# Head 0's operands loaded during the scan, and fewer, alternating visits for the triangular inverses

## The chip, the cores and the metric

The kernel runs on one core of a Trainium2 chip, as one program. Its engines are TensorE (PE, with its weight loads PEld), VectorE (DVE), ScalarE (ACT), GpSimd (POOL) and SyncE (SP), which here only issues DMAs. Each runs its own instructions in order and waits at semaphores for the others; DMA engines shared by all queues move the data. The metric is the device time of one execution in microseconds. Three runs of the kernel before gave 1317.60, 1318.98 and 1319.77 us; their median is 1318.98.

## The reference

One decoder layer over 1024 tokens (16 meta tokens ahead of them), of which two parts matter here: a gated delta rule with 4 heads, computed in chunks of 64 in the reference, and an attention with 8 heads and a forget gate. Both are normalized, projected together, added to the residual, and followed by a SwiGLU block.

```python
# gated delta rule, for one sequence of chunks
a_mat = where(strict, einsum("bhncd,bhnsd->bhncs", k, k) * decay * beta[..., :, None], 0.0)
sol = triangular_solve(a_mat + eye(chunk), rhs, left_side=True, lower=True, unit_diagonal=True)
u, w = sol[..., :dv], sol[..., dv:]
# then, chunk by chunk: S_t = e^{g_t} S_{t-1} + beta_t k_t (v_t - k_t^T e^{g_t} S_{t-1})^T, o_t = S_t^T q_t

# forgetting attention: softmax with the cumulative log forget gate as a bias, in blocks of 128 queries
# out = concat(gated delta heads, attention heads) @ w_out + residual, then RMSNorm, SwiGLU, residual
```

## The kernel before

The kernel works on chunks of 128 tokens (NT = 8 of them) and keeps matrix operands as pairs of a high and a low part, so that a projection is three matmuls for each block of 128 (high x high, low x high, high x low). Intermediate results go through DRAM tensors: `rec_d` holds the delta rule's operands by chunk, `k_d` and `q_d` the attention's keys and queries by pair of heads, `c_d` its cumulative gates, `h_d` the hidden rows.

The order of PE's instructions is written by hand: a planner, `PeOrder` (`od`), keeps an estimated time and a list of chains. A chain is a generator that says when it wants to go on; whenever none is due, the planner takes the next matmul of the fill. The fill is `fox`, the projections of the attention's values, keys (`pj_fk`) and queries (`pj_fq`), later the output projection of the delta heads (`wog`, function `wout_gdn`). The planner's estimates (`od.pe`, `od.on`, the constants `LV0`, `ATT0`, `LD0`, `LEAD`) only set the order; what the chip waits for is decided by semaphores. All other engines get their instructions in the order in which the program is written out.

The stages around the change, in order of time:

- `levels(hp)`, once for each pair of heads (at 306 and at 354 us): doubles triangular inverses from blocks of 32 to 64 to 128. The products of 32x32 (`py`, `pu`, L619 and L630) use tiles of the array at rows 32b and 32b + 32, for b = 0 and b = 2. Then `up2` transposes (L644) and multiplies (L646), and `up3` multiplies again (L658), each on 64 rows, for two heads and two halves of the tokens (t0 = 0 and 4). The result goes through POOL to `rec_d`.
- `scan()` (from 375 us): `meta_state`, then `chunk(t)` for 8 chunks. Each chunk loads `ra`, `rb`, `rc`, `zt` on SP (L751 to L757, two buffers each), and runs four visits of PE: `p` (L762, needs `ra` and the state), `pvn` (L771, needs `rb`), `pd` (L781) and `po` (L789 and L790, needs `rc`). Between them DVE and ACT evict. `mkv`, the meta tokens' operand, shares the buffers of `ra`.
- `chunk_out(t)`: ACT copies `po` to `oc` and squares it, DVE, POOL and DVE make the norm's factor, DVE makes `on` (L808), PE transposes it (`ot`, L814), and ACT and DVE split it into the pair that `wout_gdn` reads.
- `attention()`: for each head, `att_head(h)` loads `kk`, `sa`, `ka`, `qa`, `avt`, `vmt` on SP (L937 to L950); `scores` multiplies into `sc` (L975, L976) with DVE's row sums (L980) and ACT's exponentials behind them; `values` transposes the probabilities (`pt`) and multiplies them with the values (`po`, L1029 to L1034). The buffers of this stage are made when the scan's have been closed.
- `wout_gdn(nb, tt)`: 12 matmuls into one PSUM bank (`wog`), an addition to a residual tile `ht` on DVE (L1128), which was loaded from the input (L1125), and a store to `h_d` on POOL (L1129). The bank is one of three in turn, until the scores of the first group are done; from there to the end of attention it is a single one, since the others are needed (`rot[0] = 0`).

Every dozen or so of projections ends with an eviction by ACT and DVE into `fhl` and a store on SP (`fox_proj`, L717).

Of the kernel before, what the change touches and what calls it, by code (L numbers as in the profile page):

```python
# [9 lines left out]
F32 = mybir.dt.float32  # L10
F32R = mybir.dt.float32r
# [20 lines left out]
GRP = 4  # L32
LV0 = (76.0, 119.0)
LAT = 0.4
ATT0 = 7.0
LEAD = 0.6
NA = 6
LD0 = (4.0, 10.0, 18.0)
CO = 3.0
RES = 6  # L40
ORDER = (0, 4, 1, 5, 2, 6, 3, 7)
# [56 lines left out]
def tile_hymba_layer(ctx, tc, x, meta, attn_norm_w, w_in, conv_w, a_log, dt_bias, gdn_norm_w,  # L98
# [22 lines left out]
    def ps_t(name):  # L121
        return bank("tp", 3, name)
# [474 lines left out]
    def levels(hp):  # L597
# [15 lines left out]
        v4 = lambda ap: ap.rearrange("p (h t c) -> p h t c", h=2, t=NT)  # L613
        yield LV0[hp]
        py = v4(ps_s(f"py_{hp}"))
        for r, q, b in rq_:
            for i in range(2):
                for t in range(NT):
                    nc.tensor.matmul(py[r, i, t], na[q, i, t, r], u[q, i, t, q], start=True, stop=True,  # L619
                                     tile_position=(32 * b + 32, 32 * b))  # L620
                    od.pe(0.07)
# [2 lines left out]
            rdy = od.on("act", 0.5)  # L624
        yield rdy
        py = v4(ps_s(f"pu_{hp}"))
        for r, q, b in rq_:
            for i in range(2):
                for t in range(NT):
# [7 lines left out]
        lo, hi = slice(0, 64), slice(64, 128)  # L637
        t2s = {}

        def up2(i, t0):  # L640
            h = 2 * hp + i
            p2 = ps_s(f"py2_{h}_{t0}").rearrange("p (a t c) -> p a t c", a=2, t=4)
            for t in range(4):
                nc.tensor.transpose(p2[lo, 0, t], u[lo, i, t0 + t, lo], ident[lo, lo])  # L644
            for t in range(4):
                nc.tensor.matmul(p2[lo, 1, t], na[hi, i, t0 + t, lo], u[hi, i, t0 + t, hi],  # L646
                                 start=True, stop=True, tile_position=(64, 0))
            od.pe(0.7)
            t2 = lp.tile([64, 2, 4, 64], F32, tag="t2", bufs=2, name=f"t2_{h}_{t0}")
            nc.scalar.copy(t2, p2[lo])  # L650
            t2s[i, t0] = t2, od.on("act", 0.5)

        def up3(i, t0):
            h, ts = 2 * hp + i, slice(t0, t0 + 4)
            t2, _ = t2s[i, t0]
            p3 = ps_t(f"py3_{h}_{t0}").rearrange("p (a t c) -> p a t c", a=2, t=4)
            for t in range(4):
                nc.tensor.matmul(p3[lo, 0, t], t2[:, 0, t], t2[:, 1, t], start=True, stop=True,  # L658
                                 tile_position=(0, 0))
            od.pe(0.45)  # L660
# [6 lines left out]
        seq = [(i, t0) for i in range(2) for t0 in range(0, NT, 4)]  # L667
        for n, it in enumerate(seq):
            up2(*it)
            if n:  # L670
                yield t2s[seq[n - 1]][1]
                up3(*seq[n - 1])
                yield od.t + 0.3
        yield t2s[seq[-1]][1]
        up3(*seq[-1])
        lv_left.discard(hp)

    scc = ExitStack()
# [16 lines left out]
    def fox_load():  # L695
        if fox_ws:
            fox_w.append(win_block(*fox_ws.pop(0)))

    def fox_proj(dst, chunks, off, scale, nm):
        for b in range(2):  # L700
            w = fox_w.pop(0)
            for i in range(2):
                m = 2 * b + i
                for ci, (c0, n) in enumerate(chunks):
                    if (i, ci) == (0, 1):
                        fox_load()
# [12 lines left out]
    def scan():
        yield from meta_state()  # L720
        for t in range(NT):
            yield from chunk(t)

    def meta_state():
        mkv = sp.tile([P, 2, GH, P], F32, tag="ra", bufs=2, name="mkv")[:NM]
        nc.sync.dma_start(mkv, mkv_d.rearrange("h s a c -> s a h c"))
        yield od.t + 5.0
        ub = ak.tile([NM, GH, NM], F32, name="ubm")
# [178 lines left out]
    uctx.close()  # L907

    alc = ExitStack()
    al_ = alc.enter_context(tc.tile_pool(name="al", bufs=1))  # L910
# [5 lines left out]
    vmts = [al_.tile([P, P], F32R, name=f"vmt{i}") for i in range(2)]  # L916
    kas = [al_.tile([NA + DH, T], F32R, name=f"ka{i}") for i in range(2)]
    qas = [al_.tile([NA + DH, S], F32R, name=f"qa{i}") for i in range(2)]
    for ka, qa in zip(kas, qas):
        nc.gpsimd.memset(ka[:NA].bitcast(F32), 1.0)  # L920
        nc.gpsimd.memset(qa[:NA].bitcast(F32), -1.0)
    masks = []
    for z in [phm] + vmts:
        nc.gpsimd.memset(z.bitcast(F32), 0.0)

    t_ld = []

    def att_head(h):
        m, hb = h // 2, h % 2
        rows = slice(DH * hb, DH * hb + DH)  # L930
        kk = al_.tile([P, T], F32R, tag="kk", bufs=2, name=f"kk_{h}")
        sa = al_.tile([P, S], F32R, tag="sa", bufs=2, name=f"sa_{h}")
        ka, qa = kas[h % 2], qas[h % 2]
        tc_ = NM + P * GRP
        parts = ((slice(0, S // 2), slice(0, tc_)), (slice(S // 2, S), slice(tc_, T))) if h == 0 else (
            (slice(0, S), slice(0, T)),)
        nc.sync.dma_start(ka[3:NA].bitcast(F32), c_d[h])  # L937
        nc.sync.dma_start(qa[0:3].bitcast(F32), c_d[h, :, NM:T])
        for qc, kc in parts:
            for i in range(2):  # L940
                half = slice(DH * i, DH * i + DH)
                nc.sync.dma_start(kk[half, kc].bitcast(F32), k_d[m, rows, 0, kc])
                nc.sync.dma_start(sa[half, qc].bitcast(F32), q_d[m, i, rows, qc])
            nc.sync.dma_start(ka[NA:, kc].bitcast(F32), k_d[m, rows, 1, kc])
            nc.sync.dma_start(qa[NA:, qc].bitcast(F32), q_d[m, 0, rows, qc])
        vt = al_.tile([P, NT, P], F32R, tag="vt", bufs=2, name=f"avt_{h}")
        nc.sync.dma_start(vt.bitcast(F32), v_d[h, NM:T].rearrange("(t p) d -> p t d", p=P))
        vmt = vmts[h % 2]
        for r in (0, 32):
            nc.sync.dma_start(vmt[r:r + NM].bitcast(F32), v_d[h, 0:NM])  # L950
        t_ld.append(od.t)
        return m, rows, kk, sa, ka, qa, vt, vmt

    def scores(h, g, hd, out):
        m, rows, kk, sa, ka, qa, vt, vmt = hd
# [91 lines left out]

    def attention():
        groups = [(h, g) for h in range(FH) for g in range(NT // GRP)]
        hds, ptl, pos = {}, {}, [0.0]  # L1050

        def score_stream():
            for i, (h, g) in enumerate(groups):
# [3 lines left out]
                ptl[i] = []  # L1057
                for n, rdy in enumerate(scores(h, g, hds[h], ptl[i])):
                    pos[0] = i + n / (5, 9)[g]
                    yield max(rdy, t_ld[0] + LD0[i]) if i < len(LD0) else rdy  # L1060
            pos[0] = 1e9

        ss = score_stream()
# [600 lines left out]
```

## Time and profile before

| | before |
|---|---|
| median of 3 runs | 1318.98 us |
| the profiled execution | 1319.71 us |
| its span in the trace | 1318.0 us |
| granted clock of PE, mean | 0.997 |
| PE instructions | 7442 |
| DVE busy | 855.3 us |
| ACT busy | 545.4 us |
| POOL busy | 390.8 us |
| bytes moved by DMA | 233.88 MB |

The span is what the trace shows between the first and the last instruction; 1.7 us of the profiled execution lie around it. Lines of the profile (L619) are those of the kernel before. A row of the timeline gives start, duration, engine, line, operation, output and inputs, and how many instructions of one kind follow one another; in brackets stands the idle time ahead of it and what ended it. One matmul in float32 leaves more than one record, so that a group of 32 products of 32x32 has 64.

### The profile page before, as it was taken

Reading aid. Unit: us, or ns where it says so; the run is one execution under the profiler, and the core shown is the slowest. Engines: PE = TensorE matmul, PEld = TensorE weight load, DVE = VectorE, ACT = ScalarE, POOL = GpSimd, SP = SyncE. Lnnn points to the kernel's source line nnn. Section 1 sums busy time; section 2 is a strip of 40 time slices with the busy share of each in tenths; the row PEclk is TensorE's granted clock in tenths of the full one; section 3 lists DMA queues with packets and bytes.
Section 4 is the critical chain, followed back from the end, with each engine's and each line's share of the span. In section 5 each row is a group of like instructions: output and inputs, shape, how many; then the busy total and the mean of one; then the engine's idle time right before and its main releaser. Section 6 shows DMA issues by size and latency. Waiting matters only on the chain.

```text
span 1318.0 us, 20035 instructions
## 1 busy us (share of the span) xinstructions
PE 1294.8 (98%) x7442; PEld 1133.6 (86%) x7442; DVE 855.3 (65%) x1526; ACT 545.4 (41%) x918; POOL 390.8 (30%) x348
## 2 busy tenths in 40 slices
PE   8999999999999999999999999999999999999998
PEld 8999999899999988887777888888888888888887
DVE  6665789676337578996897665566566565355645
ACT  5543434232223367885553232333333343343332
POOL 2211423601013311113432644554334453010301
PEclk9999999999999999999999999999999999999999
DMA  6331743774479597647534555534444557955523
GB/s 227 100 100 45 207 140 112 203 225 148 144 235 323 185 250 219 163 115 228 171 133 137 186 176 184 160 133 157 157 165 155 176 194 264 405 183 180 209 74 128
DMA packets 184776, 233.88 MB, mean 177 GB/s; under 512 B 19120, under 2 KB 136872, under 8 KB 181864
## 3 DMA queue, kind: packets, MB, share of 16 engines
q1 hardware_dynamic: 181704, 223.70, 52.8%
q0 software_dynamic: 2976, 8.92, 2.3%
q8 instruction: 58, 0.95, 0.3%
q14 instruction: 38, 0.31, 0.1%
HBM read 154.91 MB, written 77.67 MB: 176 GB/s over the span
## 4 chain that ended last, share of the span: by engine, by line
PE 74%; DVE 9%; DMA 7%; issue 3%; ACT 3%; SPq 2%; POOL 1%; POOLq 0%; DVEq 0%; ACTq 0%
PE xp L1545 9%; PE yp L1545 7%; PE gb L1379 5%; PE ud L1379 5%; PE gd L1379 5%; PE ub L1379 5%; PE ga L1379 4%; PE ua L1379 4%; PE pj_fk L207 4%; PE pj_fq L207 3%; PE ue L1379 2%; PE ge L1379 2%; PE fv L207 2%; PE pt L1012 2%; PE po L1034 1%
## 5 line engine op out<-in xcount | busy, mean ns | idle before, releaser
L164 DVE TENSOR_TENSOR al_p<-ra_p,ah_p 128x2048 fp32r<-128x2048 f32 (+1 forms) x21 | 46.7, 2222 | 93.7 <-ACT ah_p L163 93.7
L163 ACT CAST ah_p<-ra_p 128x2048 fp32r<-128x2048 f32 (+1 forms) x21 | 37.1, 1766 | 105.8 <-PE xp L1545 48.5
L1545 PE MATMUL xp<-wh_p,al_p 128*128 128x512 f32 (+1 forms) x176 | 67.3, 382 | 0.0
L1545 PE MATMUL xp<-wl_p,ah_p 128*128 128x512 f32 (+1 forms) x176 | 67.3, 382 | 0.0
L1545 PE MATMUL xp<-wh_p,ah_p 128*128 128x512 f32 (+1 forms) x176 | 67.3, 382 | 0.0
L1432 POOL TENSOR_TENSOR gzw<-gzw,uzt 128x512 f32<-128x512 f32 x11 | 18.4, 1673 | 154.9 <-DVE uzt L1423 128.9
L1432 POOL TENSOR_TENSOR gxy<-gxy,uxy 128x512 f32<-128x512 f32 x22 | 38.9, 1766 | 66.1 <-DVE uxy L1423 45.8
L985 ACT ACTIVATE pr<-pr,sm 128x144 f32<-128x144 f32 (+3 forms) x64 | 50.5, 790 | 17.7 <-DVE sm L980 17.4
L1379 PE MATMUL gb<-uh_p,w_g_p 128*128 128x512 f32 x176 | 57.8, 389 | 0.0
L1379 PE MATMUL gd<-uh_p,w_g_p 128*128 128x512 f32 x176 | 57.8, 389 | 0.0
L1379 PE MATMUL ud<-uh_p,w_u_p 128*128 128x512 f32 x176 | 57.8, 389 | 0.0
L1379 PE MATMUL ub<-uh_p,w_u_p 128*128 128x512 f32 x176 | 57.8, 389 | 0.0
L164 DVE TENSOR_TENSOR w_u_p<-raw_u,w_u_p 128x512 fp32r<-128x512 f32 x42 | 42.8, 1018 | 21.6 <-ACT w_u_p L163 21.5
L164 DVE TENSOR_TENSOR pl<-pt,ph 128x512 fp32r<-128x512 f32 (+1 forms) x96 | 51.1, 553 | 2.2 <-ACT ph L163 1.6
L1379 PE MATMUL ga<-uh_p,w_g_p 128*128 128x512 f32 x160 | 52.5, 389 | 0.0
L1379 PE MATMUL ua<-uh_p,w_u_p 128*128 128x512 f32 x160 | 52.5, 389 | 0.0
L1545 PE MATMUL yp<-wh_p,ah_p 128*128 128x512 f32 x132 | 51.3, 389 | 0.0
L1545 PE MATMUL yp<-wl_p,ah_p 128*128 128x512 f32 x132 | 51.3, 389 | 0.0
L1545 PE MATMUL yp<-wh_p,al_p 128*128 128x512 f32 x132 | 51.3, 389 | 0.0
L163 ACT CAST ph<-pt 128x512 fp32r<-128x512 f32 (+1 forms) x96 | 44.9, 471 | 13.8 <-PE pt L1012 13.3
L164 DVE TENSOR_TENSOR wl_p<-rw_p,wh_p 128x2048 fp32r<-128x2048 f32 (+1 forms) x21 | 46.9, 2236 | 3.4 <-ACT wh_p L163 3.4
L163 ACT CAST w_u_p<-raw_u 128x512 fp32r<-128x512 f32 x42 | 26.1, 620 | 52.3 <-PE gd L1379 33.6
(646 smaller groups left out, 4305.4 us busy)
## 6 DMA issues: line engine op xcount, KB each, us to landing
ra_p<-ao_p SPq DMA_DIRECT2D x14, 1024.0 KB
raw_g<-in_w_gate_dram SPq DMA_DIRECT2D x22, 512.0 KB
raw_u<-in_w_up_dram SPq DMA_DIRECT2D x22, 512.0 KB
raw_d<-in_w_down_dram SPq DMA_DIRECT2D x22, 512.0 KB
wt_p<-raw_d SPq DMA_DIRECT2D x33, 256.0 KB
rw_p<-wt_p SPq DMA_DIRECT2D x8, 1024.0 KB
rw_p<-in_w_down_dram SPq DMA_DIRECT2D x6, 1024.0 KB
ao_p<-gzw SPq DMA_DIRECT2D x22, 256.0 KB
```

The source lines that it names most:

```text
L163: cast = nc.scalar.copy(dst_hi, src)
L164: tail[0] = (cast, nc.vector.tensor_sub(dst_lo, src, dst_hi.bitcast(F32)))
L207: nc.tensor.matmul(dst, a, b, start=first, stop=last)
L985: nc.scalar.activation(pr[:, :n], pr[:, :n], AF.Exp, bias=sm[:, np_ - 1:np_], scale=-1.0, accum_out=rsum[:, h, j:j + 1])
L1012: nc.tensor.transpose(pt[:rows_k, P * j:P * j + P], pts[j][0][:, c0:c0 + rows_k], ident)
L1034: nc.tensor.matmul(po[:, q], vt[:, kt], pl[:, q], start=False, stop=(kt == nk - 1))
L1379: nc.tensor.matmul(dst, a[:, c], b[:, k], start=(first and k == 0 and i == 0), stop=(k == 3 and i == 2), skip_group_check=not first)
L1432: last_mul[0] = G.tensor_tensor(gs[d], gs[d], us[d], op=ALU.mult)
L1545: nc.tensor.matmul(dst[:, n_], a[:, f, c], b[:, f, n_], start=(first and i == 0 and n == 0), stop=(i == NF - 1 and n == 2), skip_group_che ...
```

## The change

The loops over `py` and `pu` are turned round, so that the two blocks b = 0 and b = 2 of one product follow each other. `up2` and `up3` are cut into pieces: both halves of a head go in one visit, and the third-stage products of one head take turns with the second-stage products of the next. That makes three visits where five were.

Head 0's tiles get a pool of their own (`ale`), which is made together with the scan's; heads of odd number use a second one (`alo`), made after the scan. Head 0's loads are issued inside `fox_proj`, behind the store of the second pair's second chunk of queries, and no longer in halves. `mkv` takes a buffer of `rc` and not of `ra`. The planner's constants for the start of attention are smaller. Since `t_ld` is filled early now, all loads of `ht` take POOL's queue (`nc.gpsimd if t_ld else nc.sync`), of which the first were on SP before.

```diff
-ATT0 = 7.0
+ATT0 = 1.0
-LD0 = (4.0, 10.0, 18.0)
+LD0 = (0.0, 0.0, 10.0)
...
         py = v4(ps_s(f"py_{hp}"))
-        for r, q, b in rq_:
-            for i in range(2):
-                for t in range(NT):
+        for i in range(2):
+            for t in range(NT):
+                for r, q, b in rq_:
                     nc.tensor.matmul(py[r, i, t], na[q, i, t, r], u[q, i, t, q], start=True, stop=True,
                                      tile_position=(32 * b + 32, 32 * b))
...
+        heads = [[(i, t0) for t0 in range(0, NT, 4)] for i in range(2)]
+        for n in range(3):
+            new, old = heads[n] if n < 2 else (), heads[n - 1] if n else ()
+            p2s = [up2_t(*it) for it in new]
+            p3s = [ps_t(f"py3_{2 * hp + i}_{t0}").rearrange("p (a t c) -> p a t c", a=2, t=4) for i, t0 in old]
+            for g in range(2):
+                for t in range(4):
+                    if old:
+                        up3_m(*old[g], p3s[g], t)
+                    if new:
+                        up2_m(*new[g], p2s[g], t)
+                od.pe(0.3)
+            for it, p3 in zip(old, p3s):
+                up3_e(*it, p3)
+            for it, p2 in zip(new, p2s):
+                up2_e(*it, p2)
+            if new:
+                yield t2s[new[-1]][1]
...
                     last[0] = nc.sync.dma_start(dst(m)[:, :, c0 - off:c0 - off + n], hl[:, :, :n].bitcast(F32))
+                    if off and (m, ci) == (1, 2):
+                        assert csum_done
+                        hds[0] = att_head(0)
...
-        mkv = sp.tile([P, 2, GH, P], F32, tag="ra", bufs=2, name="mkv")[:NM]
+        mkv = sp.tile([P, 2, GH, P], F32, tag="rc", bufs=2, name="mkv")[:NM]
...
+    alec = ExitStack()
+    als = [alec.enter_context(tc.tile_pool(name="ale", bufs=1))]
     sp = scc.enter_context(tc.tile_pool(name="sp", bufs=1))
     cp = scc.enter_context(tc.tile_pool(name="cp", bufs=1, side="right"))
+    att_tiles(0)
...
-                    yield max(rdy, t_ld[0] + LD0[i]) if i < len(LD0) else rdy
+                    yield max(rdy, t_ld[h] + LD0[i]) if i < len(LD0) else rdy
```

`up2_t` is the transposes of the former `up2`, `up2_m` one product of it, `up2_e` its eviction by ACT; `up3_m` and `up3_e` are one product and the eviction of the former `up3`. `att_tiles(i)` makes the tiles `ka`, `qa`, `vmt` of a pool and clears them on POOL, as was done for both at once after the scan.

The first place is PE in the second pair of heads, the mixed visit of the levels. Names are tile names with the program's numbers; `py_3_0` are bank tiles for head 3, `t_2` the transposed pairs of head 2. Before, each visit holds one half of head 3 and the third stage of a half before it, and three projections stand between two visits:

```order
L644 MATMUL py_3_0_4073<-ident,u_3832 64x64 x4
L646 MATMUL py_3_0_4073<-u_3832,na_3825 64x64 x4
L658 MATMUL py_2_4_4084<-t_2_4_4057 64x64 x4
L207 MATMUL pj_fq_358_4012<-uh,wlo_fq_0_3733 128x342
L207 MATMUL pj_fq_358_4012<-uh,whi_fq_1_3738 128x342
L207 MATMUL pj_fq_358_4012<-ul,whi_fq_1_3738 128x342
L644 MATMUL py_3_4_4096<-ident,u_3832 64x64 x4
L646 MATMUL py_3_4_4096<-u_3832,na_3825 64x64 x4
L658 MATMUL py_3_0_4107<-t_3_0_4082 64x64 x4
```

Now it holds two halves, and the products take turns (the eight of the other half follow in the same way):

```order
L644 MATMUL py_3_0_4085<-ident,u_3848 64x64 x4
L644 MATMUL py_3_4_4090<-ident,u_3848 64x64 x4
L659 MATMUL py_2_0_4095<-t_2_0_4066 64x64
L649 MATMUL py_3_0_4085<-u_3848,na_3841 64x64
L659 MATMUL py_2_0_4095<-t_2_0_4066 64x64
L649 MATMUL py_3_0_4085<-u_3848,na_3841 64x64
```

The line L658 of before is L659 now, and L646 is L649; the transposes come first, for both halves.

The second place is SP where the scan begins. Before, the four loads of chunk 0 follow `mkv`, and `rb`, `rc`, `zt` and `ra` of chunk 1 come behind the stores of `c_d`:

```order
L726 DMA mkv<-mkv_d 16x8x128
L751 DMA ra_4281<-rec_d 128x1024
L753 DMA rb_4283<-rec_d 128x1024
L755 DMA rc_4285<-rec_d 128x1024
L757 DMA zt_4287<-rec_d 128x512
L854 DMA c_d<-c_4198 8x8x128
L717 DMA q_d<-fhl_fq_700_4211 128x2x340
L854 DMA c_d<-c_4198 8x8x128 x2
L855 DMA c_d<-c_4198 24x1x16
L753 DMA rb_4351<-rec_d 128x1024
L755 DMA rc_4353<-rec_d 128x1024
L717 DMA q_d<-fhl_fq_16_4240 128x2x342
```

Now a store of queries stands between `ra` and `rb` of chunk 0, and behind `zt` begin head 0's loads, first the gates, then, after another store, the rest; of these the last rows, from the second half of `kk`, and the next chunk's first are:

```order
L733 DMA kk_4345<-k_d 64x1040
L734 DMA sa_4346<-q_d 64x1024
L735 DMA ka_4184<-k_d 64x1040
L736 DMA qa_4185<-q_d 64x1024
L738 DMA avt_4355<-v_d 128x8x128
L740 DMA vmt_4183<-v_d 16x128 x2
L799 DMA ra_4397<-rec_d 128x1024
L801 DMA rb_4399<-rec_d 128x1024
L803 DMA rc_4401<-rec_d 128x1024
```

So `ra` of chunk 1 (`ra_4397`) moved from behind `zt` to behind head 0's operands.

The third place is PE in the first head, ahead of its first product with values (`po_0`). Before, 6 matmuls of one output tile stand between the last scores and it. Now 33 stand there, and the row at which the third of four output tiles begins is:

```order
L207 MATMUL wog_0_5242<-wlo_wo_01_5061,uh_p_4170 128x512
L207 MATMUL wog_0_5242<-whi_wo_01_5060,ul_p_4172 128x512
L207 MATMUL wog_0_5260<-whi_wo_00_5054,uh_p_4171 128x512
L207 MATMUL wog_0_5260<-wlo_wo_00_5055,uh_p_4171 128x512
L207 MATMUL wog_0_5260<-whi_wo_00_5054,ul_p_4173 128x512
```

The number behind `wog_0` is the output tile; 5196, 5242, 5260 and 5277 follow one another here, in one bank.

More of the change, by code (lines that the diff above doesn't have):

```diff
@@ L626, in levels @@
         py = v4(ps_s(f"pu_{hp}"))
-        for r, q, b in rq_:
-            for i in range(2):
-                for t in range(NT):
+        for i in range(2):
+            for t in range(NT):
+                for r, q, b in rq_:
                     nc.tensor.matmul(py[r, i, t], tb[r, i, t], y[r, i, t], start=True, stop=True,
@@ L638, in levels, with up2_t @@
         t2s = {}
-        def up2(i, t0):
+        def up2_t(i, t0):
             h = 2 * hp + i
@@ L644, in up2, with up2_m, up2_e, up3_m @@
                 nc.tensor.transpose(p2[lo, 0, t], u[lo, i, t0 + t, lo], ident[lo, lo])
[L645 to L649, printed above, removed]
+            od.pe(0.3)
+            return p2
+        def up2_m(i, t0, p2, t):
+            nc.tensor.matmul(p2[lo, 1, t], na[hi, i, t0 + t, lo], u[hi, i, t0 + t, hi],
+                             start=True, stop=True, tile_position=(64, 0))
+        def up2_e(i, t0, p2):
+            t2 = lp.tile([64, 2, 4, 64], F32, tag="t2", bufs=2, name=f"t2_{2 * hp + i}_{t0}")
             nc.scalar.copy(t2, p2[lo])
             t2s[i, t0] = t2, od.on("act", 0.5)
-        def up3(i, t0):
-            h, ts = 2 * hp + i, slice(t0, t0 + 4)
[L655 to L660, printed above, removed]
+        def up3_m(i, t0, p3, t):
+            t2 = t2s[i, t0][0]
+            nc.tensor.matmul(p3[lo, 0, t], t2[:, 0, t], t2[:, 1, t], start=True, stop=True,
+                             tile_position=(0, 0))
+        def up3_e(i, t0, p3):
+            h, ts = 2 * hp + i, slice(t0, t0 + 4)
             V.tensor_copy(u[lo, i, ts, hi], p3[lo, 0])
@@ L665, in up3 @@
             nc.sync.dma_start(rec_d[ts, :, 3, h].rearrange("t p c -> p t c"), ub)
[L667 to L675, printed above, removed]
+        heads = [[(i, t0) for t0 in range(0, NT, 4)] for i in range(2)]
[9 more added lines that the diff above has]
+                        up2_m(*new[g], p2s[g], t)
+                od.pe(0.3)
+            for it, p3 in zip(old, p3s):
[4 more added lines that the diff above has]
+                yield t2s[new[-1]][1]
         lv_left.discard(hp)
@@ L697, in fox_load, with att_tiles, att_head @@
             fox_w.append(win_block(*fox_ws.pop(0)))
+    t_ld, hds, fixed = [], {}, []
+    def att_tiles(i):
+        vmt = als[i].tile([P, P], F32R, name=f"vmt{i}")
+        ka = als[i].tile([NA + DH, T], F32R, name=f"ka{i}")
+        qa = als[i].tile([NA + DH, S], F32R, name=f"qa{i}")
+        nc.gpsimd.memset(ka[:NA].bitcast(F32), 1.0)
+        nc.gpsimd.memset(qa[:NA].bitcast(F32), -1.0)
+        nc.gpsimd.memset(vmt.bitcast(F32), 0.0)
+        fixed.append((ka, qa, vmt))
+    def att_head(h):
+        m, hb = h // 2, h % 2
+        rows = slice(DH * hb, DH * hb + DH)
+        al_ = als[h % 2]
+        kk = al_.tile([P, T], F32R, tag="kk", name=f"kk_{h}")
+        sa = al_.tile([P, S], F32R, tag="sa", name=f"sa_{h}")
+        ka, qa, vmt = fixed[h % 2]
+        nc.sync.dma_start(ka[3:NA].bitcast(F32), c_d[h])
+        nc.sync.dma_start(qa[0:3].bitcast(F32), c_d[h, :, NM:T])
+        for i in range(2):
+            half = slice(DH * i, DH * i + DH)
+            nc.sync.dma_start(kk[half].bitcast(F32), k_d[m, rows, 0])
+            nc.sync.dma_start(sa[half].bitcast(F32), q_d[m, i, rows])
+        nc.sync.dma_start(ka[NA:].bitcast(F32), k_d[m, rows, 1])
+        nc.sync.dma_start(qa[NA:].bitcast(F32), q_d[m, 0, rows])
+        vt = al_.tile([P, NT, P], F32R, tag="vt", name=f"avt_{h}")
+        nc.sync.dma_start(vt.bitcast(F32), v_d[h, NM:T].rearrange("(t p) d -> p t d", p=P))
+        for r in (0, 32):
+            nc.sync.dma_start(vmt[r:r + NM].bitcast(F32), v_d[h, 0:NM])
+        t_ld.append(od.t)
+        return m, rows, kk, sa, ka, qa, vt, vmt
     def fox_proj(dst, chunks, off, scale, nm):
@@ L818, in tile_hymba_layer @@
     ccol = gpool.tile([P, FH, NT], F32, name="ccol")
+    csum_done = []
     def csum():
@@ L855, in csum @@
         nc.sync.dma_start(c_d[:, :, 0:NM], c3[:FH, :, P:].bitcast(F32))
+        csum_done.append(1)
     def fox():
@@ L909, in tile_hymba_layer @@
     alc = ExitStack()
-    al_ = alc.enter_context(tc.tile_pool(name="al", bufs=1))
+    als.append(alc.enter_context(tc.tile_pool(name="alo", bufs=1)))
     atc = ExitStack()
@@ L915, in tile_hymba_layer @@
     phm = ap2.tile([P, 512], F32R, name="phm")
[L916 to L921, printed above, removed]
-    masks = []
[L923 to L952, printed above, removed]
+    att_tiles(1)
+    masks = []
+    nc.gpsimd.memset(phm.bitcast(F32), 0.0)
     def scores(h, g, hd, out):
@@ L1049, in attention @@
         groups = [(h, g) for h in range(FH) for g in range(NT // GRP)]
-        hds, ptl, pos = {}, {}, [0.0]
+        ptl, pos = {}, [0.0]
         def score_stream():
@@ L1251, in tile_hymba_layer @@
     alc.close()
+    alec.close()
     akc.close()
```

## The prediction

> **What bounds the kernel now.** I read the page's totals first, then the busy time by stretch from the triangular inverses to the first attention heads, then what TensorE (PE) waits for.
>
> ```profile
> span 1318.0 us, 20035 instructions
> ...
> PE 1294.8 (98%) x7442; PEld 1133.6 (86%) x7442; DVE 855.3 (65%) x1526; ACT 545.4 (41%) x918; POOL 390.8 (30%) x348
> ```
>
> ```profile
> 300.00:320.00 20.00, 20.00 (x254) 17.98 (x252) 15.85 (x44) 5.41 (x10) 1.58 (x4) 1.00 0.52 147
> 340.00:360.00 20.00, 20.00 (x225) 19.54 (x224) 4.44 (x6) 4.99 (x8) 0.00 (x0) 1.00 0.40 134
> 460.00:480.00 20.00, 18.83 (x103) 15.13 (x102) 13.64 (x46) 11.02 (x27) 3.84 (x7) 1.00 1.07 281
> ```
>
> ```profile
> PE sc L975 <- DMA qa<-c_d: 1.0, 1, 1.0
> PE sc L975 <- DVE sm L980: 0.9, 1, 0.9
> ```
>
> The columns of the second fence are the stretch, its length, the busy time of PE, its weight loads, DVE, ACT and POOL, the granted clock, the DMA share and GB/s. PE is busy 20.00 of 20.00 us around both levels and 18.83 where attention begins. So this part of the program is as long as PE's work plus its few waits, of which the third fence names the largest there. A shorter PE visit shortens the span one for one; loads, DVE and POOL count only where they come later than PE asks.
>
> **The levels: fewer and shorter visits.** PE in the first pair of heads, each visit between two projection matmuls (`pj_fk`):
>
> ```profile
> 305.82 0.32 PE L207 MATMUL pj_fk<-uh,whi_fk 128*128 128x346 f32 x1
> 306.07 2.11 PE L619 MATMUL py<-u,na 32*32 32x32 f32 x64
> 308.11 0.43 PE L207 MATMUL pj_fk<-ul,whi_fk 128*128 128x346 f32 x1
> 308.37 0.32 PE L207 MATMUL pj_fk<-uh,wlo_fk 128*128 128x346 f32 x1
> ...
> 313.77 0.32 PE L207 MATMUL pj_fk<-ul,whi_fk 128*128 128x348 f32 x1
> 314.02 0.41 PE L644 MATMUL py<-ident,u 64*64 64x64 f32 x4
> 314.36 0.67 PE L646 MATMUL py<-u,na 64*64 64x64 f32 x8
> 314.97 0.41 PE L644 MATMUL py<-ident,u 64*64 64x64 f32 x4
> ...
> 316.18 0.32 PE L207 MATMUL pj_fk<-uh,whi_fk 128*128 128x348 f32 x1
> ...
> 317.31 0.32 PE L207 MATMUL pj_fk<-uh,wlo_fk 128*128 128x348 f32 x1
> 317.47 0.32 PE L207 MATMUL pj_fk<-uh,whi_fk 128*128 128x348 f32 x1
> ...
> 318.06 0.50 PE L646 MATMUL py<-u,na 64*64 64x64 f32 x5
> 318.35 0.27 PE L658 MATMUL py<-t 64*64 64x64 f32 x1
> 318.40 0.22 PE L646 MATMUL py<-u,na 64*64 64x64 f32 x1
> ...
> 318.95 0.42 PE L207 MATMUL pj_fk<-ul,whi_fk 128*128 128x348 f32 x1
> 319.21 0.32 PE L207 MATMUL pj_fk<-uh,wlo_fk 128*128 128x348 f32 x1
> ```
>
> Two projection matmuls in a row start 0.16 apart (317.31, 317.47). A visit costs the time between the projections around it, less 0.16 for each of the two. `py` (32x32 products): 308.37 - 305.82 - 0.32 = 2.23, of which 308.11 - 306.07 = 2.04 is 64 records, 32 ns each, and 0.2 is the change of work. `pu` has the same 64 records. The second stage has five visits: 316.18 - 313.77 - 0.32 = 2.09 for the first, 317.31 - 316.18 - 0.32 = 0.81 for a lone L658, 319.21 - 317.47 - 0.32 = 1.42 for a mixed one. There are two mixed and two lone ones: 2.09 + 2 x 1.42 + 2 x 0.81 = 6.55.
>
> In the mixed visit 8 records of L646 and 8 of L658 start between 318.06 and 318.95, 0.89 us; 8 alone take 314.97 - 314.36 = 0.61. The rows at 318.35 and 318.40 show why: the two kinds, which use different rows of the array, run beside one another as soon as both are at hand. The change puts the two 32-row blocks of `py` and `pu` side by side throughout. I take each block as one stream of 32 records: 32 x 32 ns = 1.02, with the 0.2 a visit of 1.22, **1.0 less in each of four visits, -4.0**. Bounds: nothing, if the blocks exclude each other, and -4.0.
>
> The second stage becomes three visits: 0.68 of transposes (2 x 0.34, 314.02 to 314.36) and 16 records (0.61 + 8 x 0.06 = 1.09) and 0.2, 1.97; the same with L658 beside it, 1.97; 16 records alone, 1.29. That is 5.23 against 6.55, **-1.3 in each of two head pairs, -2.7** with rounding. If alternation failed, the 1.09 would come a second time in the middle visit: the bound is -0.5.
>
> A rule speaks against the first half: the Trainium skill (TensorEngine Tiling (Array Packing), Gotcha 1: PSUM Pressure) says that different row tiles cannot access the same PSUM bank at one time. Both blocks of `py` write one bank; by the rule the sum below would be 4.0 higher. The records at 318.35 and 318.40 go to two banks, so this trace neither bears it out nor refutes it.
>
> **Head 0's loads ahead of chunk 1's.** Every DMA of the head counts: 3 x (64x1040) + 3 x (64x1024) + 128x8x128 floats and small ones are 2.1 MB, and they stand on SP ahead of `ra` of chunk 1.
>
> ```profile
> 381.65 1.04 PE L732 MATMUL pvm<-mkv,ubm 16*16 16x128 f32 x8
> 386.18 1.05 PE L762 MATMUL p<-s_m,ra 128*128 128x128 f32 x8
> 393.48 1.16 PE L762 MATMUL p<-s,ra 128*128 128x128 f32 x8
> ```
>
> ```profile
> 376.00:392.00 16.00, 16.00 (x111) 14.88 (x111) 3.92 (x12) 4.67 (x9) 1.04 (x1) 1.00 0.94 307
> 388.00:392.00 4.00, 4.00 (x33) 4.00 (x32) 1.36 (x4) 2.04 (x3) 0.00 (x0) 1.00 1.03 381
> 460.00:476.00 16.00, 14.98 (x77) 11.66 (x75) 10.86 (x34) 8.74 (x20) 3.84 (x7) 1.00 1.07 259
> ```
>
> ```profile
> ra<-rec_d SPq DMA_DIRECT2D x3, 512.0 KB
> ```
>
> The DMA engines are full (0.94) at 307 GB/s where the scan begins; where a head's 64-row loads run they are full at 259. In the new order the store of the projection ahead (chunk at 16) stands before `rb` of chunk 0, so the loads start about 2.4 us (estimate: eviction by ACT and DVE, store) after its last matmul. From there to `p_1` PE has 58 projection matmuls (58 x 0.16 = 9.3) and the scan's visits: 386.18 - 381.65 less 14 matmuls = 2.3, and 393.48 - 386.18 less 18 = 4.4. Together 16.0, less 2.4: 13.6. In that time must pass: rb, rc (0.5 each), zt (0.25), a store (0.35), `ra` of chunk 1 (0.5), 2.1 MB at 307 GB/s, 6.8; the head's 2.1 MB at 259, 8.1; and 1.5 or so for issue and first bytes (estimate), 16.4. **PE waits about 3 at `p_1`.** At the 381 GB/s of 388 to 392 throughout, 11.0 and 1.5, it would be nothing; with each later chunk late by half as much again and more, 6. I take 3, since both rates are those of full engines in rows of this stage and of these loads.
>
> Such a wait has a second price:
>
> ```profile
> 240.62 0.27 PE L466 MATMUL prk<-ident,rk 128*8 128x128 f32 x1 [1.96 <-POOL rk L463]
> ```
>
> ```profile
> 241.00:244.30 3.30, 3.30 (x16) 3.30 (x17) 3.30 (x9) 2.57 (x4) 3.30 (x2) 0.50 0.48 63
> ```
>
> After 1.96 us without work the granted clock was 0.50 for 3.3 us. Half of 3.3 is **+1.7**, if the wait lasts as long as that one did; 0 if it stays shorter. The Trainium skill (TensorE: Matmul & The Clock Gate, What's actually happening) puts the fall after about 3.4 us of idling; by that the 1.7 would not be paid and the sum would end 1.7 lower. Here the row shows a shorter idle time that was followed by it, so I keep the price.
>
> **The end of the scan.** Less fill is left there.
>
> ```profile
> 443.40 0.39 PE L790 MATMUL po<-vn,rc 128*128 128x128 f32 x2
> ```
>
> ```profile
> 447.72 1.14 DVE L808 SCALAR_TENSOR_TENSOR on<-oc,os,zt 128x128 f32<-128x128 f32 x4
> ...
> 450.07 1.29 DVE L164 TENSOR_TENSOR wlo_wo<-raw_wo,whi_wo 128x512 fp32r<-128x512 f32 x2 [0.79 <-ACT whi_wo L163]
> ```
>
> From the last `po` to the end of `on` go 447.72 + 1.14 - 443.40 = 5.5 us, all behind projections before. Now 26 projections (4.2) and `ot_6` (some 0.5, as its transposes alone need over 0.34) stand before `ot_7`, and one pair of weight splits (1.29) has moved ahead of `on` on DVE. If the chain stays as it is, PE waits 5.5 - 4.7 = 0.8; with all of the 1.29, 2.1, and with ACT's casts ahead too, some 2.6. I take **+1.7**, nearer the upper end, since ACT's and DVE's splits are both in the chain.
>
> **One bank for four output tiles.** Ahead of `po_0` PE now has 33 `wog` matmuls in a row, over three tile boundaries, at a point where the rotation of banks is off: each boundary waits for the addition of the tile before.
>
> ```profile
> 454.23 0.39 PE L207 MATMUL wog<-whi_wo,ul_p 128*128 128x512 f32 x1
> ...
> 454.66 0.69 DVE L1128 TENSOR_TENSOR ht<-wog,ht 128x512 f32<-128x512 f32 x1 [0.41 <-PE wog L207]
> ```
>
> Before, the next `wog` began at 454.46, 0.23 later, beside the addition. Now it begins after 0.43 + 0.69, so 0.9 is lost, **three times, +2.7**. Nothing, if what comes behind (`po_0`) is late anyway; 4.4, if a score's DVE work of 0.57 stands ahead of each addition. I take the plain chain.
>
> **Head 1's wait goes:** -1.0 (third fence), since its loads now come while head 0 computes. What is late next there is DVE's softmax, as in the 0.9 beside it; the bound is nothing.
>
> **The residual tiles `ht`** are now all loaded through POOL's queue, behind the second head's memsets.
>
> ```profile
> 449.06 0.96 POOL L920 MEMSET ka<- 6x1040 f32 x1 [1.71 <-DVE on L808]
> 449.96 0.94 POOL L921 MEMSET qa<- 6x1024 f32 x1
> ```
>
> ```profile
> DMA to landing us min/median/max: 4.3/7.5/9.6
> ```
>
> These wait for `on_7`, take 1.9 and more, and a load lands 7.5 later: 9.7 after `on_7`. The first addition is due some 7 after it (5 + 7 `wog`, 2.8, four score pairs and `ot_7`); DVE, waiting in order, then holds the scores behind it, which have two or three banks in hand. Of 2.5 late, I take **+1.3** on PE; bounds 0 and 3 (landing at 4.3 and at 9.6).
>
> **Costed at nothing:** head 0's memsets, now ahead of chunk 0's work on POOL, which is busy 1.04 of the 16 us from 376 (without that cover, the 2.2 that they take); the `mkv` tile in another buffer, which adds no work; and the earlier start of attention as such, since PE's matmuls are the same ones and only change places with `wog`.
>
> **The sum**, against the profiled execution (1319.71 us; span 1318.0): -4.0 - 2.7 + 3.0 + 1.7 + 1.7 + 2.7 - 1.0 + 1.3 = +2.7. The profiled execution lies 0.7 above the median of 1318.98; on the median that is 1321.7, and I round to **1321.5**, as overlapping waits don't quite add up.
>
> **Rivals.** (1) The loads keep up: the row of 388 to 392 reaches 381 GB/s, and the head's loads may mix well with others; against it stands the 259. Then 3.0 and 1.7 go: 1318.98 - 2.0 = 1317. (2) Every new wait is covered, and the levels' gain shows: -6.7 - 1.0 and the 0.8 at the scan's end, 1318.98 - 6.9 = 1312. PE's 20.00 of 20.00 speaks for the gain, the missing fill against the cover. (3) The other side: the two 32-row blocks exclude each other in their one bank, so `py` and `pu` stay at 2.23. It decides from the point that both streams need the bank at once, which is in every record; price 4.0, 1325.5. (4) Each chunk's loads stay late, 6 instead of 3: 1324.5.
>
> **How the numbers follow.** Forecast 0.42, rivals (1) 0.20, (2) 0.14, (3) 0.13, (4) 0.11. A measurement tells 0.2%, 2.6 us, from no change: faster is below 1316.3, slower above 1321.6. The forecast's own spread (1318 to 1325) is half same, half slower; of (1) a half is faster. So faster 0.25, same 0.34, slower 0.41. The range leaves out the far half of (2) and the ends of (3) and (4): 1312 to 1326.5.
>
> **What would show it.** `py` and `pu` groups of 64 records in about 1.1 us and three visits behind them; an idle time at `p_1` with `ra` as releaser and, if over 2 us, a stretch at 0.50; an idle time at `ot_7`; three of 0.9 at `wog` boundaries, released by `ht`; no wait for `qa`. I am wrong if `p_1` starts without a wait, or if the groups keep 2.1.

## The result, and the profile after

| | before | changed |
|---|---|---|
| median of the device times | 1318.98 us (5 runs, 1317.60 to 1319.93) | 1332.02 us (5 runs, 1329.69 to 1332.89) |
| ratio, 95% interval | | 1.0094, 1.0081 to 1.0107 |
| span of the profiled execution | 1318.0 us | 1330.8 us |
| first product of the levels to last scores | 284.2 us | 298.3 us |

The change makes the kernel 0.94% slower, 13.0 us by the medians. The last line of the table, from the first `py` product to the last product with `ka` (306.07 to 590.25 us before, 305.10 to 603.41 us after), holds all of it: 14.1 us. What comes behind takes 727.8 us before and 727.4 after. This stage's time is used below beside the medians, since the part of the program before it differs by up to 2.7 us from one profiled execution to another.

PE's waits, as the page of the changed kernel groups them (engine, line, what was waited for, us in total, how often, the longest):

```profile
PE p L810 <- DMA ra<-rec_d: 9.0, 1, 9.0
PE sc L994 <- DVE sm L999: 4.5, 2, 4.2
PE wog L207 <- DVE ht L1147: 2.3, 3, 0.8
...
PE ot L862 <- DVE on L856: 0.7, 1, 0.7
```

There is no wait for `qa` any more. The levels are as short as the change meant them to be; PE's timeline of the changed kernel:

```profile
304.86 0.32 PE L207 MATMUL pj_fk<-uh,whi_fk 128*128 128x346 f32 x1
305.10 1.20 PE L619 MATMUL py<-u,na 32*32 32x32 f32 x64
306.23 0.43 PE L207 MATMUL pj_fk<-ul,whi_fk 128*128 128x346 f32 x1
306.50 0.32 PE L207 MATMUL pj_fk<-uh,wlo_fk 128*128 128x346 f32 x1
...
308.01 1.20 PE L630 MATMUL pu<-y,tb 32*32 32x32 f32 x64
...
310.99 0.32 PE L207 MATMUL pj_fk<-ul,whi_fk 128*128 128x348 f32 x1
311.24 0.63 PE L644 MATMUL py<-ident,u 64*64 64x64 f32 x8
311.80 1.14 PE L649 MATMUL py<-u,na 64*64 64x64 f32 x16
...
313.15 0.32 PE L207 MATMUL pj_fk<-uh,whi_fk 128*128 128x348 f32 x1
...
314.42 0.32 PE L207 MATMUL pj_fk<-uh,wlo_fk 128*128 128x348 f32 x1
315.13 0.89 PE L644 MATMUL py<-ident,u 64*64 64x64 f32 x8 [0.39 <-ACT t L654]
315.95 0.27 PE L659 MATMUL py<-t 64*64 64x64 f32 x1
315.96 0.27 PE L649 MATMUL py<-u,na 64*64 64x64 f32 x1
...
317.30 0.32 PE L207 MATMUL pj_fk<-ul,whi_fk 128*128 128x348 f32 x1
```

The 64 records of `py` take 1.20 us where they took 2.11, and the third-stage product starts 0.01 us from a second-stage one. The visit costs 306.50 - 304.86 - 0.32 = 1.32. Counted in the same way, the second stage has visits of 1.84, 2.56 (with a wait of 0.39 for ACT) and 1.25 us in the first pair and of 1.83, 1.83 and 1.25 in the second. With `py` and `pu` both pairs come to 15.9 us, where they took 22.0: 6.2 less, or 6.6 without that wait.

The 9.0 us stand at the first product of chunk 1. SP's queue and PE there:

```profile
377.91 0.44 SPq L762 DMA_DIRECT2D q_d<-fhl_fq  x1
378.40 0.47 SPq L801 DMA_DIRECT2D rb<-rec_d  x1
...
381.11 0.53 SPq L733 DMA_DIRECT2D kk<-k_d  x1
...
387.73 2.49 SPq L740 DMA_DIRECT2D vmt<-v_d  x2
391.06 0.34 SPq L799 DMA_DIRECT2D ra<-rec_d  x1
```

```profile
398.63 2.05 PE L810 MATMUL p<-s,ra 128*128 128x128 f32 x8 [9.01 <-DMA ra<-rec_d]
...
407.90 1.06 PE L810 MATMUL p<-s,ra 128*128 128x128 f32 x8
```

`ra` of chunk 1 is asked for ten us behind `kk`, when PE already waits (since 389.62), and comes 7.6 us later. The eight records of `p` then take 2.05 us instead of 1.06, and chunk 2 begins 9.3 us after chunk 1, where a chunk lasts 7.3: the clock was halved. The stretches of that time (length, busy PE, PEld, DVE, ACT, POOL, granted clock, DMA share, GB/s):

```profile
384.00:386.00 2.00, 2.00 (x17) 2.00 (x16) 1.52 (x5) 1.46 (x3) 0.00 (x0) 1.00 1.04 393
386.00:394.00 8.00, 3.62 (x31) 3.43 (x29) 2.80 (x6) 1.74 (x3) 2.07 (x2) 0.91 1.06 216
396.00:400.00 4.00, 1.36 (x6) 1.40 (x7) 0.00 (x0) 0.00 (x0) 0.00 (x0) 0.50 1.02 398
398.60:402.60 4.00, 3.96 (x16) 4.00 (x17) 1.84 (x8) 0.00 (x0) 0.00 (x0) 0.50 1.04 402
468.70:474.20 5.50, 5.50 (x18) 4.52 (x19) 3.20 (x10) 2.70 (x6) 0.86 (x2) 0.50 1.04 236
```

From 386 to 394, where head 0's keys, queries and values move, the DMA engines are full at 216 GB/s; around it they are full at nearly 400. The half clock lasts about 4.0 us of work after the first long wait and 5.5 us after the second, which is worth 2.0 and 2.75 us.

The second wait, on POOL, DVE and PE:

```profile
456.57 1.62 POOL L983 TENSOR_SCALAR_AFFINE_SELECT zmask<-zmask 128x128 f32<-128x128 f32 x1
458.14 0.96 POOL L717 MEMSET ka<- 6x1040 f32 x1
...
460.10 2.94 POOL L1144 DMA_DIRECT2D ht<-in_x_dram  x5
```

```profile
467.48 0.69 DVE L1147 TENSOR_TENSOR ht<-wog,ht 128x512 f32<-128x512 f32 x1 [4.37 <-DMA ht<-in_x_dram]
```

```profile
468.70 0.69 PE L994 MATMUL sc<-ka,qa 70*128 70x392 f32 x1 [4.19 <-DVE sm L999]
```

The page names the softmax on DVE (L999) as what PE waited for; DVE itself had stood 4.37 us at the addition in front of it, for a load issued at 460.10. That is the case of a name which is not the cause.

The account of the stage. Waits: +9.0 at chunk 1, +3.6 at the scores (4.5 for DVE, where 0.9 was before), +2.3 at the output tiles, +0.7 at `ot_7`, +0.4 for ACT in the levels, -1.0 for head 1's wait, together 15.0. Half clocks: +2.0 and +2.75. The level visits without their wait: -6.6. That makes 13.2 of the 14.1 us measured; 0.9 us are not placed.

### The profile page after: what moved, and what is told of

It reads as the page before. It is cut to its first block, busy times and chain, and to the rows that moved or that the text cites. A ratio compares the mean times of both kernels' runs of the same rounds, so it can differ in the third digit from the quotient of the medians.

```text
span 1330.8 us, 20025 instructions
## 1 busy us (share of the span) xinstructions
PE 1291.6 (97%) x7442; PEld 1130.9 (85%) x7442; DVE 857.5 (64%) x1526; ACT 545.4 (41%) x918; POOL 391.0 (29%) x350
## 4 chain that ended last, share of the span: by engine, by line
PE 74%; DMA 8%; DVE 8%; issue 3%; ACT 3%; SPq 2%; POOL 1%; POOLq 0%; DVEq 0%; ACTq 0%
PE xp L1565 8%; PE yp L1565 7%; PE gb L1399 5%; PE ub L1399 4%; PE ud L1399 4%; PE gd L1399 4%; PE ga L1399 4%; PE ua L1399 4%; PE pj_fk L207 2%; PE ge L1399 2%; PE ue L1399 2%; PE pj_fq L207 2%; PE pt L1031 2%; PE wog L207 2%; PE po L1053 1%
```

## The experiments

Each ratio is to the kernel before on the same chip, whose medians there were 1318.98 to 1320.68 us; it is not the quotient of two medians. Stage is again first `py` to last product with `ka`, of the profiled execution.

| run | median, us | ratio to before, 95% interval | stage, us |
|---|---|---|---|
| changed kernel | 1332.02 | 1.0094, 1.0081 to 1.0107 | 298.3 |
| e1_levels | 1324.94 | 1.0029, 1.0013 to 1.0045 | 290.9 |
| e2_after_chunk1 | 1328.96 | 1.0064, 1.0041 to 1.0086 | 294.4 |
| e3_ht_sync | 1327.32 | 1.0054, 1.0039 to 1.0068 | 290.7 |
| e4_end_ht | 1318.81 | 0.9988, 0.9971 to 1.0005 | 281.4 |
| e5_wide | 1426.82 | 1.0807, 1.0779 to 1.0835 | |
| e6_v_late | 1330.98 (one run) | | 294.1 |
| e7_ld | 1315.32 | 0.9967, 0.9954 to 0.9980 | 278.4 |
| e8_wide_ld | 1412.93 | 1.0703, 1.0680 to 1.0726 | |
| e9_pairs | 1330.91 | 1.0084, 1.0070 to 1.0099 | 293.8 |
| e10_pairs_ld | 1314.67 | 0.9957, 0.9942 to 0.9971 | 281.0 |
| e11_old_levels | 1319.17 | 0.9990, 0.9976 to 1.0004 | 284.9 |

**The levels alone.** The function `levels` of the changed kernel in the kernel before.

```diff
-        for r, q, b in rq_:
-            for i in range(2):
-                for t in range(NT):
+        for i in range(2):
+            for t in range(NT):
+                for r, q, b in rq_:
...
-        seq = [(i, t0) for i in range(2) for t0 in range(0, NT, 4)]
+        heads = [[(i, t0) for t0 in range(0, NT, 4)] for i in range(2)]
...
```

> The kernel before with the new levels alone (loop order of the 32x32 products and three visits where there were five); loads, constants and queues stay as before. Theory A (the two blocks run side by side and three visits are cheaper, each us on PE counts in full): 6.7 us less than before, 1312.3. Rival B (the blocks exclude each other in their one PSUM bank): 2.7 less, 1316.3. Rival C (the gain is given back later, because the scan then asks for its loads earlier than they come): within 1.5 of before, with a new wait at a chunk's first product.

It is slower than before by 0.29%. Rival C, and by more than I gave it. PE's two largest waits there:

```profile
PE sc L987 <- DMA qa<-q_d: 5.2, 3, 4.4
PE p L774 <- DMA ra<-rec_d: 2.9, 1, 2.9
```

PE now arrives earlier at chunk 1's operand and at head 1's, and waits 2.9 and 4.4 us, each with a half clock behind it. In the kernel before, chunk 1's operand came without a wait and head 1's 1.0 us late, so the shorter levels show first as waits for DMAs.

**Only the order of head 0 and chunk 1.**

```diff
-                    if off and (m, ci) == (1, 2):
-                        assert csum_done
-                        hds[0] = att_head(0)
...
         nc.sync.dma_start(zt, rec_d[t, :, 7])
+        if t == NT - 1:
+            assert csum_done
+            hds[0] = att_head(0)
```

> The changed kernel with head 0's loads written in the scan's last chunk instead of behind the store of the queries; by the order of SP they then stand behind the loads of chunk 1 and ahead of those of chunk 2, nothing else moves. Theory A (the 9.0 us at the first product of chunk 1 are the time that 2.1 MB of head 0 take ahead of its operand): that wait goes, and since a chunk lasts 7.3 us, 1.7 to 2 come back at the first product of chunk 2; too short to halve the clock, so 9.0 + 1.4 - 1.9 = 8.5 less than the changed kernel, 1323.5. Rival B (the wait comes from the start of the scan, where chunk 0's second operand now stands behind a store of queries): 4 us or more stay at chunk 1, 1327 or above.

```profile
PE p L810 <- DMA ra<-rec_d: 5.2, 1, 5.2
```

Chunk 1 begins on time (389.7) and chunk 2 waits 5.2 us, where I had expected 1.9; the ratio gives 4.0 us less than the changed kernel instead of 8.5. Theory A holds as to the place: the wait is where head 0's bytes are, and rival B is out. Why my size was wrong was not tried apart; the likely reason is that the rest of chunk 1's operands (1.25 MB) now stand ahead of chunk 2 as well, some 3.3 us at 380 GB/s (estimate). A chunk's 1.75 MB every 7.3 us and the stores leave little room, and 2.1 MB more were late at both places that were tried.

**The residual tiles on SP.**

```diff
-            (nc.gpsimd if t_ld else nc.sync).dma_start(ht, x[cols, nbc])
+            (nc.gpsimd if len(t_ld) > 1 else nc.sync).dma_start(ht, x[cols, nbc])
```

> The changed kernel with the loads of the residual tiles on SP's queue until the second head's operands are asked for (the first three tiles; the later ones stay on POOL's). Theory A (the 4.2 us at the scores are the landing of the first tile, asked for behind the second head's memsets on POOL): that wait goes, and with it the half clock behind it, 1.7: 5.9 less than the changed kernel, 1326.1. Rival B (the softmax on DVE is late by itself): a wait of 2 us or more stays at the scores, 1329 or above.

```profile
PE sc L994 <- DVE sm L999: 1.6, 2, 1.3
```

The long wait went from 4.2 to 1.3 us, and the ratio fell by 0.40%, 5.3 us (5.9 expected). Theory A. The stage is 7.6 us shorter, but not by this wait alone: the wait at chunk 1 was 6.5 us here and not 9.0. In this execution the clock was halved at the scan's start, with PE busy without a break ahead of it, so that PE came about 1.6 us later to the operand:

```profile
380.00:382.00 2.00, 2.00 (x15) 1.79 (x14) 0.00 (x0) 0.54 (x1) 0.00 (x0) 1.00 1.04 302
382.20:385.50 3.30, 3.30 (x14) 3.30 (x14) 1.23 (x1) 1.63 (x2) 1.04 (x1) 0.50 0.96 251
```

What halved it there no run shows.

**Both, with head 0 behind the scan's last load.**

```diff
-        nc.sync.dma_start(zt, rec_d[t, :, 7])
+        zt_ld = nc.sync.dma_start(zt, rec_d[t, :, 7])
+        if t == NT - 1:
+            with tc.issue_after(zt_ld.ins):
+                hds[0] = att_head(0)
```

> The changed kernel with head 0's loads behind the last load of the scan, where the DMA engines of the kernel before stood idle (438 to 450 us), and with the residual tiles as in the run before this. Theory A (the waits of the changed kernel are these two and their half clocks, and everything else of the change is as it was costed): 9.0 + 1.4 + 4.2 + 1.7 = 16.3 less than the changed kernel, 1315.7, with the waits at output tiles (2.3) and at the last transposes (0.7) still there. Rival B (the loads in the idle stretch come too late for the first scores): a wait for a DMA at the first scores of 2 us or more, 1318 or above. Rival C (the time moves to another wait, as the fill runs out earlier): 1319 and above without a DMA wait.

No wait for a DMA is left in the stage, which is 16.9 us shorter than that of the changed kernel (16.3 expected); by the ratios it is 14.0 us. Rival B is out, and the stage speaks for theory A; the median, 1318.81, lies between A's 1315.7 and rival C's 1319. Left are the output tiles and the last transposes:

```profile
PE wog L207 <- DVE ht L1147: 2.4, 3, 0.8
...
PE ot L862 <- DVE on L856: 0.7, 1, 0.7
```

Head 0's loads run alone now, and are no faster for it:

```profile
436.00:444.00 8.00, 8.00 (x61) 7.99 (x60) 5.23 (x16) 3.57 (x8) 1.40 (x2) 1.00 1.01 215
```

But not all of them are slow. The first half of `kk`, 64 rows to 64 partitions like the others, moves at 358 GB/s until the next load joins it:

```profile
436.50:437.00 0.50, 0.50 (x6) 0.50 (x5) 0.50 (x2) 0.00 (x0) 0.00 (x0) 1.00 0.89 358
437.50:438.00 0.50, 0.50 (x6) 0.50 (x6) 0.45 (x3) 0.02 (x1) 0.00 (x0) 1.00 1.05 213
```

**One DMA over both halves.** Two kernels changed the loads of `kk` and `sa`.

```diff
-        for i in range(2):
-            half = slice(DH * i, DH * i + DH)
-            nc.sync.dma_start(kk[half].bitcast(F32), k_d[m, rows, 0])
-            nc.sync.dma_start(sa[half].bitcast(F32), q_d[m, i, rows])
+        nc.sync.dma_start(kk.bitcast(F32), k_d[m, rows, 0][None].broadcast_to([2, DH, T]))
+        nc.sync.dma_start(sa.bitcast(F32), q_d[m, :, rows])
```

> The changed kernel with each head's kk and sa loaded by one DMA over 128 partitions each instead of two over 64; bytes, places and order stay. In the changed kernel a 4 KB packet of a head's loads took 0.29 to 0.33 us while one of the scan's loads took 0.16. Theory A (a load over 64 partitions moves at half the rate): the packets of kk and sa fall to 0.16, 256 packets on 16 engines save 2.2 us, the wait at the first product of chunk 1 falls from 9.0 to about 6.8, and later heads' data come earlier: 1329 or 1330 against 1332.0. Rival B (the rate is set by the source, or by what else runs): packets stay at 0.3 and the wait at 8.5 to 9.5.

A miss: neither theory is tested, and the kernel is 8% slower.

```profile
387.00:394.00 7.00, 4.13 (x35) 3.94 (x33) 3.32 (x6) 2.08 (x4) 1.42 (x2) 0.97 0.13 53
```

The DMA share is 0.13, as much as two engines of sixteen: the two halves were the outer step of the source. The Trainium skill (DMA: Bandwidth & Descriptors, Rules for kernel authors) says that an outermost dimension smaller than 16 confines a DMA to that many engines; the trace agrees. The same loads in e7_ld, told below, gave 1412.93 us:

> The run before with kk and sa of every head loaded by one DMA over 128 partitions each. If loads over 64 partitions are slow as such, heads' data land 2 us earlier: no DMA wait in attention, and 0 to 1 us less than the run before. If not, equal to it.

So the source was turned round, to pairs of rows as the outer step:

```diff
+        nc.sync.dma_start(kk.bitcast(F32), k_d[m, rows, 0:1].broadcast_to([DH, 2, T]))
+        nc.sync.dma_start(sa.bitcast(F32), q_d[m, :, rows].rearrange("i p c -> p i c"))
```

> The changed kernel with kk and sa of each head loaded by one DMA each that walks 64 pairs of rows over 128 partitions, so that all 16 DMA engines work and reach all partitions (the run with two halves as the outer step kept only two engines busy and told nothing of the rate). Rows of kk and sa are paired in another order, which their sum doesn't see. Theory A (loads that fill only 64 partitions move at half the rate): packets of kk and sa take 0.16 us where they took 0.3, 16 packets on each engine save 2.2 us, the wait at the first product of chunk 1 is 6.5 to 7 instead of 9.0, and the kernel 1329 to 1330. Rival B (the rate is the source's): 0.3 us for a packet, a wait of 8.5 to 9.5.

```profile
386.00:390.00 4.00, 4.00 (x34) 4.00 (x33) 2.66 (x5) 1.81 (x3) 0.00 (x0) 1.00 1.07 344
390.00:394.00 4.00, 1.08 (x10) 0.89 (x8) 1.12 (x4) 1.22 (x2) 1.47 (x2) 0.99 1.07 216
```

In the first of these rows `kk` and `sa` move (with the rest of a store) at 344 GB/s and full share; a 4 KB packet took 0.16 us there, against 0.29 to 0.33 in the changed kernel. In the second come `ka` and `qa`, still on 64 rows, and the values: 216 again. The packets are as theory A has them. That the number of partitions is the cause is not shown by it, as the order of the rows changed too, and the first half of `kk` in e4_end_ht was fast on 64. The wait fell to 7.1 us, and from the issue of `kk` to chunk 1's product went 15.8 us instead of 17.5. But e3_ht_sync, whose loads there are those of the changed kernel, had 16.6 and a wait of 6.5, so that such a time differs by a us between executions, and the ratio (1.0084 against 1.0094) tells nothing.

**The values later.** Of head 0, `avt` and `vmt` behind the scan's last load, keys and queries in their place.

```diff
+            with tc.issue_after(zt_ld.ins):
+                v_late[0]()
```

> The changed kernel with head 0's value loads (0.53 MB in 512-byte packets, and the two small ones) behind the scan's last load; its keys and queries stay where they are. Theory A (the wait is the time of the packets ahead of chunk 1's operand): 1024 packets of 0.05 us on 16 engines are 3.2 us, the wait falls from 9.0 to 5.8. Rival B (SP is the limit, which could not issue for 2.5 us at the last small load, not the packets): it falls by under 1. Rival C (only bytes count, at the mean 205 GB/s of that stretch): by 2.6.

```profile
PE p L820 <- DMA ra<-rec_d: 6.7, 1, 6.7
```

The wait is 2.3 us shorter, and from the issue of `kk` to chunk 1's product went 14.8 us, 2.7 less than in the changed kernel and 1.8 less than in e3_ht_sync. The wait fell by more than the 1 us that I gave rival B; but SP's stop of 2.5 us at `vmt` was moved away together with the packets, so the run doesn't part the two. Nor does it tell 3.2 by packets from 2.6 by bytes.

**Fewer output matmuls in a row.** To e4_end_ht, the planner's delay:

```diff
-LD0 = (0.0, 0.0, 10.0)
+LD0 = (0.0, 0.0, 3.0)
```

> The kernel with head 0's loads in the idle stretch and the first residual tiles on SP, and the planner's delay for head 1's scores cut from 10 to 3: 10 output matmuls and one tile boundary stand ahead of the first product with values instead of 33 and three. Theory A (each boundary on the one bank costs the 0.8 that the trace shows): 1.6 less, and the matmuls moved into later heads fill gaps there, 0.5 to 1 more: 1316.5 where the run before was 1318.8. Rival B (head 1's data are not there yet): a DMA wait at head 1's first scores takes the gain back, 1318.5 or above.

```profile
PE sc L994 <- DVE sm L999: 1.3, 2, 1.1
...
PE wog L207 <- DVE ht L1147: 0.9, 1, 0.9
```

One wait of 0.9 where three made 2.4; stage 278.4 us, 3.0 less than e4_end_ht, in one execution of each; the intervals of the two ratios overlap. It beats both kernels: 0.9967 of the kernel before, 0.9954 to 0.9980. The block of 33 came from that constant: it is counted from the moment when head 1's loads are issued, and the planner filled the time with `wog`.

> The fastest run so far (head 0's loads in the idle stretch, first residual tiles on SP, head 1's delay cut to 3) with the paired loads of the run before for every head. Theory A: a head's data land 2 us earlier; the DMA wait at head 1 is gone already, so 0 to 1 us less than that run, 1314.5 to 1315.5. Rival B: equal to it.

The paired loads on top of it give 0.9957, 0.9942 to 0.9971; the intervals overlap, and whether it is faster than e7_ld stays open. In its profiled execution the first scores wait 2.2 us for DVE, with a half clock behind it, which hides what the loads may have brought to the stage:

```profile
PE sc L992 <- DVE sm L997: 2.4, 2, 2.2
```

**The old levels in the fastest kernel.**

```diff
-        heads = [[(i, t0) for t0 in range(0, NT, 4)] for i in range(2)]
+        seq = [(i, t0) for i in range(2) for t0 in range(0, NT, 4)]
...
```

> The fastest run so far with the old levels (old loop order, five visits), everything else as there. Theory A (once no load is waited for, PE's time in the levels counts in full): 5.5 to 6.7 more than that run, 1321 to 1322, so that the moves of the loads alone are worth nothing or less against the kernel before. Rival B (the levels' gain is hidden or given back here too, as in the run with the levels alone): within 2 of that run.

The stage is 284.9 us against 278.4, 6.5 more. Not all of it is the levels: in this execution PE waited 1.5 us at an output tile, and the clock was halved a little later, which costs 1.65 of the 3.30 us of work below and did not happen in e7_ld's stage.

```profile
PE wog L207 <- DVE ht L1135: 1.5, 1, 1.5
```

```profile
469.70:473.10 3.40, 3.30 (x11) 2.94 (x12) 1.31 (x6) 1.24 (x5) 0.55 (x1) 0.50 1.09 315
```

That leaves 4.8 us, just under theory A's 5.5 to 6.7 and far from rival B's 2. By the ratios the difference is 0.23%, 3.0 us, with intervals that allow about 0.5 to 5.5: the runs say that the levels are worth something here, not how much. Without them the moves of the loads are worth nothing that can be measured (0.9990, 0.9976 to 1.0004).

## Why the prediction was wrong, step by step

The forecast was 1321.5 with a range up to 1326.5. Every wait that it named came, at the place it named; the sizes of two were far off, and the price of the half clock was counted once where it came twice.

- **Levels, -6.7.** Right: `py` and `pu` cost 1.32 for 1.22 forecast, and both pairs come out at -6.6 by their own rows; a wait of 0.4 for ACT in the middle visit was not in the sum. Rival (3), the shared bank, is refuted by the 1.20 us of `py` and `pu`; with it falls the Trainium skill's rule (TensorEngine Tiling (Array Packing), Gotcha 1: PSUM Pressure) for this case.
- **Chunk 1's operand, 3.0.** The failed step, 9.0 measured. It had two halves. I let 13.6 us pass from the first `rb` load to `p_1`; it was 389.62 - 378.40 = 11.2, since the store ahead of `rb` went 3 us later than its data: it stood on SP behind the loads and stores of `mkv`, `ra` and `c_d`. And I took 16.4 us for the data; it was 398.63 - 378.40 = 20.2. The 259 GB/s for a head's loads came from a row of 16 us in which other loads ran too; alone they make 215. By that rate the 2.1 MB take 9.8 us and not 8.1 (estimate), which is 1.7 of the 3.8 that I was short; where the other 2.1 went no run shows, though SP itself stood 2.5 us at the last small load (the row of `vmt`). My bound of 6 rested on the 259 as well.
- **The half clock, 1.7.** Right in kind, 2.0 there. But the same price, 2.75, came a second time at the scores, where I had not asked whether the wait was long enough.
- **The residual tiles, 1.3.** The second failed step, 4.2 measured. The load landed 7.4 us after its issue (7.5 taken), but the issue itself came 3.3 us after `on_7`, since `zmask`'s two instructions stood before the memsets too. And I let the scores' banks absorb half of DVE's delay, where PE waited 4.19 of DVE's 4.37.
- **The output tiles, 2.7,** measured 2.3; **the end of the scan, 1.7,** measured 0.7, near the lower bound of 0.8; **head 1's wait, -1.0,** gone as said.

With the sizes that the rows show, the account above comes to 13.2 of the 14.1 us; the forecast's own terms had come to 2.7.

## What to carry to other kernels

A rate for a load that is moved comes from a stretch in which that kind of load runs alone, not from a row in which it runs among faster ones. Before work is made earlier or shorter, look at what arrives just in time beside it: here 6 us of saved PE time alone made the kernel slower, and they paid only when the loads had been put into a stretch where the DMA engines stood idle. In a stage of full DMA engines, moving bytes forward moved the wait, and in this stage each wait of PE of 2.2 us and more was charged twice, by the clock.

## What the runs showed of the hardware

- A head's loads, most of them 64 rows of 4 KB to 64 partitions each, moved at 215 GB/s with all DMA engines full; with `kk` and `sa` over 128 partitions, in pairs of rows, it was 344. The second run read the same rows of the source, so that the rate hangs on the partitions, or on the order in which they are walked; the two were not tried apart. A first load to 64 partitions at 358 GB/s, in e4_end_ht, shows that their number alone doesn't set it.
- The idle time of about 2 us ahead of `prk` (1.6 to 2.1 in eleven profiled executions, e5_wide and e8_wide_ld left out) was followed by a halved clock in eight of them and not in three, among these the changed kernel with 2.13, the longest. All of PE's waits of 2.2 us and more in the stage were, none of 1.3 us and less; the one of 1.5, in e11_old_levels, was, and in e3_ht_sync a half clock came with no wait ahead of it. The Trainium skill (TensorE: Matmul & The Clock Gate, What's actually happening) has a window of 3.4 us that runs freely; that one and the same wait is charged in one execution and not in the next agrees with it, that it takes a whole idle window does not, and these 1.7 us are part of the spread between runs.
- In `py` and `pu` two row blocks that write one bank ran side by side: 64 records in 1.20 us, where one block at a time took 2.11.
